# First layer of a two-layer trunk: where the convolution's taps read, who makes the first of them, and which PSUM banks the gate projection uses

## The chip, the cores and the metric

One core of a Trainium2 chip runs the whole program in one launch. Its engines work side by side, each through its own list of instructions in order: TensorE (PE, matmuls), VectorE (DVE), ScalarE (ACT), GpSimd (POOL), and SyncE (SP), whose queue issues the DMAs. SBUF is the on-chip memory, and matmul results land in PSUM, which has eight banks of 128 x 512 float32. GpSimd's operations of this kernel work in SBUF alone. The metric is the device time of one execution in microseconds (us); the figure that counts is the median of the runs.

## The reference

The input is 2048 frames of 1024 channels. The first layer is a gated linear recurrence, the second a gated delta rule; each has a norm scaled by a conditioning vector before it and a gated residual behind it. The change touches the first layer only, but for where one constant is made:

```python
def rglru_block(h, in_w, conv_w, conv_b, gate_w, gate_b, lam, out_w):
    proj = h @ in_w                                   # 1024 -> 2 x 1024
    xb, zg = proj[..., :D_RNN], proj[..., D_RNN:]
    xb = causal_dwconv(xb, conv_w) + conv_b           # 4 taps along the frames, each channel by itself
    ...
    pre = jnp.einsum('bsni,knij->kbsnj', xg, gate_w)  # 8 blocks of 128 x 128, two gates
    ...
    y = hseq.astype(h.dtype) * jax.nn.silu(zg)
    return y @ out_w
```

`causal_dwconv` pads three zero frames on the left, so that frame t takes channels of frames t-3 to t.

## The kernel before

**Tiling.** Everything is float32. Channels lie on the 128 partitions, frames along the free dimension. The frames go in two halves `u` of 1024, each in two pieces `i` of 512. A projection weight panel is 1024 x 128 (eight tiles `k`). Weights and activations are split into two parts (`whi`, `wlo`; `hh`, `hl`), and a product takes three passes, so a job (one panel, one piece) is 24 matmuls of 128 x 512 into one PSUM bank (`products`, L667). The first layer has 16 panels: for each block `n` of 128 channels an `x` panel (goes through the convolution) and a `z` panel (the gate projection of the change: SiLU of it multiplies the branch). For a block the jobs run x i=0, x i=1, z i=0, z i=1.

**The convolution** (`conv1_thread`, with `extend` and `taps`): ACT copies the bank into an SBUF tile `xe` of 4 + 512 columns (L727); POOL fills the first four from the piece before (`carry`, L725, or zeros, L721) and saves the last four (L730); POOL makes the first tap with the bias (L741); DVE adds the other three taps (L715). Then `gates_thread`: ACT rounds `xf` to `xh` (L765), DVE makes the rest `xl` (L768), PE multiplies both with the gate weights (`pg`, L774, six matmuls for a piece), ACT and DVE make the gates (L824, L784 to L801), DVE scans along the frames (L805), POOL multiplies by `tz` (L812), which `z1_thread` made (ACT L750, DVE L752).

**PSUM.** Eight banks, two to a tag: `mm` (all projections), `tp` (transposes), `c` (gates), `d` (transposes of the first two pieces, then idle until the second layer's recurrence).

**What sets the order.** A planner (`Weave`) runs threads written as generators. A thread yields what it needs: an event, a buffer slot (`slots[...]`), or an engine for an estimated time (`STT` 0.665 us for a tap, `EV` 0.605, `CP` 0.48). The planner always lets the thread go on that can start earliest by these estimates, and the instructions are issued in that order on each engine. Estimates decide only the order; on the chip each engine follows its list and waits on semaphores. Between the first layer's work lie other threads: norms of the second half (L452 to L459, POOL L245, L246), its transposes by DVE (L506), conditioning rows (DVE L412, `acc`), the split of weights on POOL (L649, `wlo`). At about 505 us the output projection (`mmo`) begins, at 696 us the second layer's projections.

**The second layer's** convolution uses the same `extend` and `taps` and isn't changed. `middle` is a 128 x 128 constant for its decay sums.

## Time and profile before

| | |
|---|---|
| three runs | 1982.22, 1986.4, 1989.81 us; median 1986.4 |
| profiled execution | 1980.38 us, span of its instructions 1978.6 us |
| PE busy | 1846.2 us (93%), 10286 matmuls |
| DVE busy | 1475.7 us (75%) |
| ACT busy | 1046.7 us (53%) |
| POOL busy | 724.1 us (37%) |
| first layer's projections | about 50 to 516 us |
| output projection of the first layer | to 696 us |
| second layer | to the end |

Busy is the time in which an engine has an instruction in work. A busy PE is not PE at its peak: its matmuls are pipelined, and one at the lower clock counts as longer. "PEclk" is the granted share of PE's full clock. An idle gap before an instruction is put down to the engine whose semaphore came last. `xt_d`, `araw`, `raw` and the like are DMA targets of other threads.

### The profile page before, as it was taken

What the parts mean: (1) busy time and instruction counts of PE and PEld (TensorE: products, weight loads), DVE (VectorE), ACT (ScalarE), POOL (GpSimd) and SP (SyncE); (2) the same over time, 40 slices, a digit from 0 to 9 for tenths busy, and PEclk for the clock granted to TensorE, in tenths of its full rate; (3) what the DMA queues carried; (4) which work ended last, traced back from release to release, by engine and by line L of the source; (5) the groups of instructions that cost most, each with busy time, mean ns of one, the idle gap of its engine ahead of it and who ended that gap; (6) DMA issues with size and microseconds to landing.
All of it is one profiled execution on the core that took longest, in us unless ns stands there. A gap on an engine that the chain in (4) does not pass through costs nothing.

```text
span 1978.6 us, 31398 instructions
## 1 busy us (share of the span) xinstructions
PE 1846.2 (93%) x10286; PEld 1500.3 (76%) x10286; DVE 1475.7 (75%) x3171; ACT 1046.7 (53%) x2555; POOL 724.1 (37%) x1215
## 2 busy tenths in 40 slices
PE   6998889999998998898989999999999999999998
PEld 3776667787787777777777778777888888878887
DVE  6788798887644567778977898567778778877654
ACT  3655567666411236465555555555656566654321
POOL 4555664444200135345344544333333334311101
PEclk9999999999999999999999999999999999999999
DMA  8355655654578724547764457455465555577751
GB/s 334 103 157 158 223 168 169 200 178 153 175 198 210 225 74 140 145 114 176 189 161 130 119 125 191 128 147 147 119 152 147 131 133 140 149 219 221 225 186 64
DMA packets 511724, 322.77 MB, mean 163 GB/s; under 512 B 371268, under 2 KB 439236, under 8 KB 511560
## 3 DMA queue, kind: packets, MB, share of 16 engines
q1 hardware_dynamic: 511560, 320.77, 57.4%
q8 instruction: 81, 1.33, 0.3%
q14 instruction: 83, 0.68, 0.1%
HBM read 219.93 MB, written 100.73 MB: 162 GB/s over the span
## 4 chain that ended last, share of the span: by engine, by line
PE 46%; DVE 21%; DMA 10%; issue 6%; ACT 6%; POOL 5%; SPq 5%; DVEq 0%; POOLq 0%; ACTq 0%
PE mm L667 21%; PE mmo L667 12%; DVE xf L715 6%; DMA raw<-in_w 2%; DVE ttmp L1249 2%; DVE tblk L1252 2%; PE pg L774 1%; DMA xt<-x_d 1%; SPq L1187 1%; SPq L512 1%; DVE acc L412 1%; PE pp L1369 1%; PE pS L1398 1%; PE pkk L1129 1%; PE pS L1399 1%
## 5 line engine op out<-in xcount | busy, mean ns | idle before, releaser
L715 DVE SCALAR_TENSOR_TENSOR xf<-xe,cw_s,xf 128x512 f32<-128x512 f32 x384 | 331.4, 866 | 46.7 <-POOL xf L958 24.1
L649 POOL TENSOR_TENSOR wlo<-raw,whi 128x1024 fp32r<-128x1024 f32 x48 | 120.6, 2512 | 99.7 <-ACT whi L643 81.2
L1249 DVE TENSOR_TENSOR ttmp<-blk,tblk 128x60 f32<-128x60 f32 (+24 forms) x496 | 118.3, 238 | 24.9 <-DMA blk<-blk_d 11.5
L643 ACT CAST whi<-raw 128x1024 fp32r<-128x1024 f32 x96 | 100.4, 1045 | 64.5 <-DMA raw<-in_w 54.7
L1252 DVE TENSOR_TENSOR tblk<-tblk,ttmp 128x60 f32<-128x60 f32 (+24 forms) x496 | 122.3, 247 | 10.0 <-POOL tblk L1243 0.2
L730 POOL COPY carry<-xe 128x4 f32<-128x4 f32 x128 | 40.3, 315 | 239.2 <-ACT xe L727 237.1
L727 ACT COPY xe<-mm 128x512 f32<-128x512 f32 x128 | 73.9, 578 | 74.0 <-PE mm L667 73.0
L667 PE MATMUL mm<-hh_('in2', 0)_5201,whi 128*128 128x512 f32 x256 | 105.0, 410 | 4.1 <-ACT xe L727 4.1
L667 PE MATMUL mmo<-oh,yh 128*128 128x512 f32 x256 | 101.1, 395 | 7.8 <-DVE xr L922 7.2
L667 PE MATMUL mm<-hh_('in2', 1)_12203,whi 128*128 128x512 f32 x256 | 105.2, 411 | 2.8 <-ACT xe L727 2.8
L667 PE MATMUL mm<-hh_('in2', 0)_5424,whi 128*128 128x512 f32 x256 | 103.7, 405 | 2.1 <-ACT xe L727 1.5
L667 PE MATMUL mm<-hh_('in2', 0)_5201,wlo 128*128 128x512 f32 x256 | 105.3, 411 | 0.0
L667 PE MATMUL mm<-hl_('in2', 0)_5425,whi 128*128 128x512 f32 x256 | 104.9, 410 | 0.0
L667 PE MATMUL mm<-hl_('in2', 0)_5202,whi 128*128 128x512 f32 x256 | 104.6, 409 | 0.0
L667 PE MATMUL mm<-hh_('in2', 1)_12379,wlo 128*128 128x512 f32 x256 | 104.4, 408 | 0.0
L667 PE MATMUL mm<-hh_('in2', 1)_12203,wlo 128*128 128x512 f32 x256 | 104.4, 408 | 0.0
L667 PE MATMUL mm<-hh_('in2', 0)_5424,wlo 128*128 128x512 f32 x256 | 104.0, 406 | 0.0
L667 PE MATMUL mm<-hl_('in2', 1)_12204,whi 128*128 128x512 f32 x256 | 103.8, 405 | 0.0
L667 PE MATMUL mm<-hl_('in2', 1)_12380,whi 128*128 128x512 f32 x256 | 103.2, 403 | 0.0
L667 PE MATMUL mm<-hh_('in2', 1)_12379,whi 128*128 128x512 f32 x256 | 103.1, 403 | 0.0
L667 PE MATMUL mmo<-oh,oh 128*128 128x512 f32 (+1 forms) x264 | 102.0, 386 | 0.2 <-DVE tz L986 0.2
L667 PE MATMUL mmo<-ol,oh 128*128 128x512 f32 (+1 forms) x264 | 102.1, 387 | 0.0
(324 smaller groups left out, 5698.7 us busy)
## 6 DMA issues: line engine op xcount, KB each, us to landing
raw<-in_w SPq DMA_DIRECT2D x96, 512.0 KB, 4.2
araw<-in_ada_w SPq DMA_DIRECT2D x32, 512.0 KB, 4.4
xt<-x_d SPq DMA_DIRECT2D x32, 512.0 KB, 4.5
xt_d<-xb SPq DMA_DIRECT2D x192, 64.0 KB, 2.6
xk<-xt_d SPq DMA_DIRECT2D x24, 512.0 KB, 5.5
xt<-in_x SPq DMA_DIRECT2D x16, 512.0 KB, 4.9
ada<-in_ada_w SPq DMA_DIRECT2D x16, 512.0 KB, 9.1
y_d<-tz SPq DMA_DIRECT2D x32, 256.0 KB, 3.1
```

What stands on the lines that cost most here:

```text
L412: dve.scalar_tensor_tensor(acc, raw[:, k, :], ck, acc, ALU.mult, ALU.add)
L512: sp.dma_start(out=dst[c_], in_=tb[32 * c_:32 * c_ + 32])
L643: act.copy(hi, raw)
L649: pool.tensor_tensor(lo, raw, f(hi), ALU.subtract)
L667: pe.matmul(pt, lhsT=lhs[a][:, k, :], rhs=rhs[b][:, k, :], start=(k == 0 and n == 0), stop=(k == KT - 1 and n == 2))
L715: dve.scalar_tensor_tensor(xf, xe[:, 1 + j:1 + j + TC], wc[:, j:j + 1], xf, ALU.mult, ALU.add)
L727: act.copy(xe[:, 4:4 + TC], pt)
L730: pool.tensor_copy(out=carry, in_=xe[:, TC:TC + 4])
L774: pe.matmul(pg, lhsT=a[:, g, :], rhs=b, start=(q == 0), stop=(q == 2))
L1129: pe.matmul(pkk[:, b, :], lhsT=kc, rhs=kc, start=True, stop=True)
L1249: dve.tensor_tensor(tmp, blk[:, j, j + 1:32].unsqueeze(2).to_broadcast([P, r, c_]), t[:, j, 0:c_].unsqueeze(1).to_broadcast([P, r, c_]), A ...
L1252: dve.tensor_tensor(t[:, j + 1:32, 0:c_], t[:, j + 1:32, 0:c_], tmp, ALU.subtract)
```

## The change

A new function `convolve` takes the place of `extend`, POOL's first tap and `taps` in the first layer. ACT makes the tap that needs no earlier frame (the last weight, with the bias) straight from PSUM into `xf`, for the columns 3 to 511. It then copies the first three and the last three columns of the bank into a small buffer `edge1`, six columns for each piece and channel block. DVE adds the other three taps from PSUM into columns 3 to 511; the bank is free after the third. The first three columns of the piece come apart, from the six edge columns that lie side by side in `edge1`: one product of 3 x 4, one sum over 4, one addition of the bias. `xe1` and `carry1` go; the rounding `xh`, which shared `xe1`'s buffers, gets its own tag `xh`. The `z` jobs of the first layer take the tag `d` in place of `mm`. `middle` is made when the second layer's buffers are opened, no longer at the start.

```diff
-    middle = cp.tile([P, P], F32, name="middle")
-    pool.tensor_copy(out=middle, in_=upper)
-    pool.tensor_scalar(middle[0:64, :], middle[0:64, :], -1.0, 0.0, ALU.add, ALU.add)
...
-        mtok = yield slots["mm"]
-        pt = ps.tile([P, TC], F32, tag="mm", name="mm")
+
+        bank = "d" if layer == 1 and kind == "z" else "mm"
+        mtok = yield slots[bank]
+        pt = ps.tile([P, TC], F32, tag=bank, name="mm")
...
-    def conv1_thread(u, n, i, pt, mtok):
-        etok = yield slots["xe1"]
-        xe = tile_([P, TC + 4], "xe1", "xe1")
+    def window(ap, *steps):
+        return bass.AP(ap.tensor, ap.offset, [ap.ap[0], *steps])
+
+    def convolve(xf, pt, mtok, wc, bias, edge, key, g, bank):
+
+
+        yield "act", 0.66 if bias is not None else 0.57, 0.0
+        if bias is None:
+            act.activation(xf[:, 3:TC], pt[:, 3:TC], AF.Copy, scale=wc[:, 3:4])
+        else:
+            act.activation(xf[:, 3:TC], pt[:, 3:TC], AF.Identity, bias=bias, scale=wc[:, 3:4])
+        yield "act", 0.18, 0.1
+
+        if g < S // TC - 1:
+            act.copy(edge[:, 6 * g + 3:6 * g + 9].rearrange("p (a b) -> p a b", b=3), window(pt[:, 0:3], (TC - 3, 2), (1, 3)))
+        else:
+            act.copy(edge[:, 6 * g + 3:6 * g + 6], pt[:, 0:3])
+        w.set(ev("edge", key, g))
+        for j in range(3):
+            yield "dve", STT, 0.13 if j < 2 else 0.05
+            dve.scalar_tensor_tensor(xf[:, 3:TC], pt[:, j:j + TC - 3], wc[:, j:j + 1], xf[:, 3:TC], ALU.mult, ALU.add)
+        put(bank, mtok)
+        if g > 0:
+            yield ev("edge", key, g - 1)
+        etok = yield slots["ed"]
+        yield "dve", 0.09, 0.1
+        pr = tile_([P, 3, 4], "ed", "ed")
+        dve.tensor_tensor(pr, window(edge[:, 6 * g:6 * g + 3], (1, 3), (1, 4)), wc.unsqueeze(1).to_broadcast([P, 3, 4]),
+                          ALU.mult)
+        yield "dve", 0.09, 0.1
+        dve.tensor_reduce(out=xf[:, 0:3], in_=pr, axis=mybir.AxisListType.X, op=ALU.add)
+        if bias is not None:
+            yield "dve", 0.14, 0.1
+            dve.tensor_scalar(xf[:, 0:3], xf[:, 0:3], bias, None, ALU.add)
+        put("ed", etok)
+
+    def conv1_thread(u, n, i, pt, mtok, bank):
         yield ev("columns")
-        yield from extend(xe, pt, mtok, carry1[:, n, :], ("x", n), u * NTC + i)
         ftok = yield slots["xf1"]
-        yield "pool", 0.76
         xf = tile_([P, TC], "xf1", "xf1")
-        pool.tensor_scalar(xf, xe[:, 1:1 + TC], cw1_s[:, n, 0:1], cb1_s[:, n:n + 1], ALU.mult, ALU.add)
-        yield from taps(xe, xf, cw1_s[:, n, :])
-        put("xe1", etok)
+        yield from convolve(xf, pt, mtok, cw1_s[:, n, :], cb1_s[:, n:n + 1], edge1[:, n, :], ("x", n), u * NTC + i, bank)
...
+        middle = tile_([P, P], "middle", "middle")
+        pool.tensor_copy(out=middle, in_=upper)
+        pool.tensor_scalar(middle[0:64, :], middle[0:64, :], -1.0, 0.0, ALU.add, ALU.add)
+        w.set(ev("middle"), middle)
         w.set(ev("l2"))
...
+        edge1 = tile_([P, KT, 6 * (S // TC)], "edge1", "edge1")
+        pool.memset(edge1, 0.0)
```

The new estimates make the planner order the whole first layer anew. Three places follow. Lines of the changed kernel differ from those of before (L663 for L667, L751 for the taps L715, L796 for `xl` L768, L802 for L774, L820 for L792, L840 for L812, L489 for L493).

On DVE, the two pieces of block 2 of the first half; of before, `xf_1041` and `xf_1077` are the pieces i=0 and i=1, `xb` is a transpose of the second half's frames:

```order
L715 SCALAR_TENSOR_TENSOR xf_1041<-xe_992,cw_s,xf_1041 128x512
L801 TENSOR_TENSOR tg<-tg 128x512
L715 SCALAR_TENSOR_TENSOR xf_1041<-xe_992,cw_s,xf_1041 128x512
L805 SCALAR_TENSOR_TENSOR tg<-th,hcar,tg 128x512
L715 SCALAR_TENSOR_TENSOR xf_1041<-xe_992,cw_s,xf_1041 128x512
L715 SCALAR_TENSOR_TENSOR xf_1077<-xe_1048,cw_s,xf_1077 128x512
L506 STREAM_TRANSPOSE xb<-xt 128x512
L715 SCALAR_TENSOR_TENSOR xf_1077<-xe_1048,cw_s,xf_1077 128x512
L768 TENSOR_TENSOR xl<-xf_1041,xh 128x512
L715 SCALAR_TENSOR_TENSOR xf_1077<-xe_1048,cw_s,xf_1077 128x512
```

Of the changed kernel, the same pieces are `xf_1009` and `xf_1064`; `ed` is the product of the edge columns:

```order
L751 SCALAR_TENSOR_TENSOR xf_1009<-mm,cw_s,xf_1009 128x509 x3
L758 TENSOR_TENSOR ed<-edge_123,cw_s 128x12
L761 TENSOR_REDUCE xf_1009<-ed 128x3
L764 TENSOR_SCALAR xf_1009<-xf_1009,cb_s 128x3
L829 TENSOR_TENSOR tg<-tg 128x512
L833 SCALAR_TENSOR_TENSOR tg<-th,hcar,tg 128x512
L751 SCALAR_TENSOR_TENSOR xf_1064<-mm,cw_s,xf_1064 128x509
L796 TENSOR_TENSOR xl<-xf_1009,xh 128x512
L751 SCALAR_TENSOR_TENSOR xf_1064<-mm,cw_s,xf_1064 128x509 x2
L758 TENSOR_TENSOR ed<-edge_123,cw_s 128x12
L761 TENSOR_REDUCE xf_1064<-ed 128x3
```

The three taps of i=0 stand together, the edge operations follow them, and `xl` of i=0 stands behind one tap of i=1 in place of two taps and a transpose.

On POOL at the same two pieces, before (`tz` is the last product of an earlier piece, `wlo` the split of a panel):

```order
L649 TENSOR_TENSOR wlo<-raw_938,whi 128x1024
L730 COPY carry_103<-xe_992 128x4
L741 TENSOR_SCALAR xf_1041<-xe_992,cw_s,cb_s 128x512
L725 COPY xe_1048<-carry_103 128x4
L808 COPY hcar<-tg 128x1
L842 TENSOR_TENSOR gl<-gw,gh 128x256
L812 TENSOR_TENSOR tz<-tz,tg 128x512
L730 COPY carry_103<-xe_1048 128x4
L741 TENSOR_SCALAR xf_1077<-xe_1048,cw_s,cb_s 128x512
L808 COPY hcar<-tg 128x1
L812 TENSOR_TENSOR tz<-tz,tg 128x512
```

And of the changed kernel, the same stretch:

```order
L645 TENSOR_TENSOR wlo<-raw_953,whi 128x1024
L836 COPY hcar<-tg 128x1
L840 TENSOR_TENSOR tz<-tz,tg 128x512
L870 TENSOR_TENSOR gl<-gw,gh 128x256
L836 COPY hcar<-tg 128x1
L840 TENSOR_TENSOR tz<-tz,tg 128x512
L645 TENSOR_TENSOR wlo<-raw_1068,whi 128x1024
L241 TENSOR_SCALAR ss<-ss 128x1
```

No operation of the convolution is left on POOL between the `wlo` of two panels; the others stay.

On PE at the layer's start, where the second piece's frames are transposed (`tph`) between the first products; before, the places around the first gate products (`pg`):

```order
L493 MATMUL tph<-ident,xt 128x128 x4
L667 MATMUL mm<-hl_('in1', 0)_481,whi 128x512
L667 MATMUL mm<-hh_('in1', 0)_480,wlo 128x512
L667 MATMUL mm<-hh_('in1', 0)_480,whi 128x512
L667 MATMUL mm<-hl_('in1', 0)_481,whi 128x512
L667 MATMUL mm<-hh_('in1', 0)_480,wlo 128x512
L667 MATMUL mm<-hh_('in1', 0)_480,whi 128x512
L667 MATMUL mm<-hl_('in1', 0)_481,whi 128x512
L667 MATMUL mm<-hh_('in1', 0)_480,wlo 128x512
L774 MATMUL pg<-xh,gh 128x512
L774 MATMUL pg<-xl,gh 128x512
L774 MATMUL pg<-xh,gl 128x512
```

And of the changed kernel:

```order
L663 MATMUL mm<-hh_('in1', 0)_471,whi 128x512
L663 MATMUL mm<-hl_('in1', 0)_472,whi 128x512
L663 MATMUL mm<-hh_('in1', 0)_471,wlo 128x512
L489 MATMUL tph<-ident,xt 128x128 x12
L802 MATMUL pg<-xh,gh 128x512
L802 MATMUL pg<-xl,gh 128x512
L802 MATMUL pg<-xh,gl 128x512
L489 MATMUL tph<-ident,xt 128x128 x4
L802 MATMUL pg<-xh,gh 128x512
L802 MATMUL pg<-xl,gh 128x512
L802 MATMUL pg<-xh,gl 128x512
L489 MATMUL tph<-ident,xt 128x128 x4
```

Before, the last group of four transposes stood behind the 55th product of the layer. Now 20 transposes stand behind the 57th, with the first gate products between them, because these transposes take turns on the banks `tp` and `d`, and the first `z` job holds one of `d`.

From the first jobs of the output projection on, the rows of all engines stand as before but for a few: the two operations for `middle` on POOL, and a single product or pair of products on PE that changes places with a neighbour.

## Rows read from the trace of the kernel before

**Rows 1.** Stretches of the span: busy us (instructions) of each engine, PEclk, DMA share, GB/s.
```profile
50.00:100.00 50.00, 46.26 (x212) 36.55 (x212) 39.91 (x53) 32.02 (x47) 26.47 (x31) 0.99 0.38 103
100.00:350.00 250.00, 219.65 (x894) 172.86 (x893) 211.54 (x245) 157.82 (x217) 143.00 (x138) 0.95 0.57 176
350.00:450.00 100.00, 98.04 (x440) 80.06 (x439) 87.53 (x112) 65.58 (x87) 45.17 (x52) 1.00 0.56 179
450.00:516.00 66.00, 64.01 (x274) 50.71 (x272) 51.05 (x60) 42.05 (x53) 29.53 (x31) 1.00 0.48 158
516.00:696.00 180.00, 170.66 (x734) 137.78 (x733) 93.04 (x128) 42.34 (x53) 18.91 (x26) 0.99 0.72 207
696.00:1979.00 1283.00, 1217.02 (x7639) 1004.32 (x7637) 959.85 (x2502) 688.06 (x2070) 439.61 (x904) 0.99 0.56 149
```

**Rows 2.** What PE waited for, 100 to 350 us: us in total, times, longest.
```profile
PE pg L774 <- DVE xl L768: 20.0, 8, 5.2
...
PE mm L667 <- DVE tz L752: 0.4, 1, 0.4
```

**Rows 3.** Chain of waits, 119 to 137 us: start us, us, what.
```profile
117.70 1.70 POOL tz L812
...
120.00 2.28 POOL xf L741
...
126.93 0.61 DVE xl L768
...
129.24 1.28 PE pg L774 x3
...
133.55 0.70 PE pg L774 x3
```

**Rows 4.** Instructions in order of time, DVE and then POOL: start us, us, operation.
```profile
122.30 1.87 DVE L715 SCALAR_TENSOR_TENSOR xf<-xe,cw_s,xf 128x512 f32<-128x512 f32 x1 [0.51 <-POOL xf L741]
...
124.73 2.21 DVE L715 SCALAR_TENSOR_TENSOR xf<-xe,cw_s,xf 128x512 f32<-128x512 f32 x1
...
127.46 0.74 DVE L715 SCALAR_TENSOR_TENSOR xf<-xe,cw_s,xf 128x512 f32<-128x512 f32 x1
...
123.59 2.79 POOL L649 TENSOR_TENSOR wlo<-raw,whi 128x1024 fp32r<-128x1024 f32 x1
```

**Rows 5.** Taps and `tz`, 50 to 516 us: ns min/median/max, first and last start.
```profile
L715 DVE SCALAR_TENSOR_TENSOR xf<-xe,cw_s,xf x96: 705/752/2896, 58.4 to 507.7; 128x512 f32<-128x512 f32 x96
...
L752 DVE SCALAR_TENSOR_TENSOR tz<-tz,mm x32: 655/680/690, 61.4 to 507.1; 128x512 f32<-128x512 f32 x32
```

**Rows 6.** DVE's groups, 100 to 350 us: busy us, mean ns, idle before and releaser.
```profile
L715 DVE SCALAR_TENSOR_TENSOR xf<-xe,cw_s,xf 128x512 f32<-128x512 f32 x48 | 53.0, 1105 | 8.0 <-POOL xf L741 7.7
L412 DVE SCALAR_TENSOR_TENSOR acc<-araw,c_col,acc 128x512 f32<-128x512 f32 x24 | 23.3, 973 | 1.4 <-DMA araw<-in_ada_w 1.2
L794 DVE SCALAR_TENSOR_TENSOR tg<-tg,xf 128x512 f32<-128x512 f32 x17 | 18.6, 1094 | 0.0
...
L752 DVE SCALAR_TENSOR_TENSOR tz<-tz,mm 128x512 f32<-128x512 f32 x17 | 11.6, 681 | 8.4 <-ACT tz L750 5.6 <-issue 2.8
```

**Rows 7.** POOL's groups, 50 to 516 us, columns as in rows 6.
```profile
L741 POOL TENSOR_SCALAR xf<-xe,cw_s,cb_s 128x512 f32<-128x512 f32 x32 | 40.1, 1254 | 0.8 <-DVE tg L794 0.6
...
L730 POOL COPY carry<-xe 128x4 f32<-128x4 f32 x32 | 15.7, 492 | 16.9 <-ACT xe L727 16.7
...
L725 POOL COPY xe<-carry 128x4 f32<-128x4 f32 x24 | 13.0, 542 | 2.2 <-DVE xf L715 2.2
```

**Rows 8.** ACT's groups: 40 to 520 us, and the last row the whole span.
```profile
L727 ACT COPY xe<-mm 128x512 f32<-128x512 f32 x32 | 18.7, 583 | 44.8 <-PE mm L667 44.6
...
L562 ACT ACTIVATE h<-tph,cond 128x512 f32<-128x512 f32 x12 | 8.7, 776 | 10.8 <-DVE cond L271 6.7 <-PE tph L493 3.0 <-POOL hl_('in1', 0)_481 L573 1.1
...
L1030 ACT COPY ab<-pb 128x64 f32<-128x64 f32 x4 | 0.8, 204 | 2.2 <-PE pb L1027 2.2
```

**Rows 9.** A small DVE operation, 50 to 516 us, columns as in rows 6.
```profile
L274 DVE SCALAR_TENSOR_TENSOR cond<-cond,norm_s 128x4 f32<-128x4 f32 x2 | 0.3, 160 | 0.0
```

More of the change, by code (lines that the diff above doesn't have):

```diff
@@ L193, in trunk_kernel @@
     dtb_s = cp.tile([P, NH], F32, name="dtb_s")
-    carry1 = cp.tile([P, KT, 4], F32, name="carry1")
     hcar = cp.tile([P, KT], F32, name="hcar")
@@ L210, in trunk_kernel @@
         "gs": 2, "eg": 2}.items()}
-    for t in ("xe", "xf", "vt", "ec", "gr", "ab", "gin", "gg", "spe", "spd"):
+    for t in ("xe", "xf", "vt", "ec", "gr", "middle", "ab", "gin", "gg", "spe", "spd"):
         tags[t] = ("l2a", tags[t][1])
@@ L685, in job @@
         if layer == 1:
-            w.spawn((conv1_thread if kind == "x" else z1_thread)(u, m, i, pt, mtok), 2, 0.2)
+            w.spawn((conv1_thread if kind == "x" else z1_thread)(u, m, i, pt, mtok, bank), 2, 0.2)
         elif kind == "z":
@@ L744, in conv1_thread, with z1_thread @@
         w.set(ev("xf", u, n, i), (xf, ftok))
-    def z1_thread(u, n, i, pt, mtok):
+    def z1_thread(u, n, i, pt, mtok, bank):
         ztok = yield slots["tz"]
@@ L752, in z1_thread @@
         dve.scalar_tensor_tensor(tz, tz, 1.0, pt, ALU.add, ALU.mult)
-        put("mm", mtok)
+        put(bank, mtok)
         w.set(ev("tz", u, n, i), (tz, ztok))
@@ L758, in gates_thread @@
         gh, gl = yield ev("gw", u, n)
-        etok = yield slots["xe1"]
+        etok = yield slots["xh"]
         ltok = yield slots["xr"]
@@ L763, in gates_thread @@
         yield "act", CP
-        xh = tile_([P, TC], "xe1", "xh", F32R)
+        xh = tile_([P, TC], "xh", "xh", F32R)
         act.copy(xh, xf)
@@ L775, in gates_thread @@
             w.spawn(gate_thread(u, n, i, g, pg, ctok), 3)
-        put("xe1", etok)
+        put("xh", etok)
         put("xr", ltok)
@@ L1045, in decay_thread @@
         yield "pe", 1.1
+        middle = yield ev("middle")
         pgc = ps.tile([P, 3, NB * NH], F32, tag="tp", name="pgc")
```

7 lines of the change are left out of this document (4 added, 3 removed).

## Prediction

> **What bounds the kernel now.** I read the busy times in stretches first [rows 1]. The change touches only the first layer's projections, 50 to 516 us; the question there is how fast TensorE (PE) issues. From 350 to 450 us it issues 440 matmuls in 100 us, 4.40 per us, at full granted clock. At that rate the 894 matmuls of 100 to 350 us need 203.2 us, so that stretch loses 46.8 of its 250 us; the 212 of 50 to 100 need 48.2 (1.8 lost), the 274 of 450 to 516 need 62.3 (3.7 lost). All the change can win here is about 52 us. Behind 516 us the instructions stand as before on every engine (but for a few rows), so those 1460 us are taken as unchanged.
>
> What costs the 46.8 us? In PE's waits [rows 2], gate products waiting for `xl` on VectorE (DVE) are the one large entry, 20.0 us in 8 waits, 2.5 us each. The rest is mostly what follows them: in the chain of waits [rows 3] the gate products after such a wait take 0.43 us each (1.28 for three), and 4 us later 0.23 (0.70 for three), which are TensorE's two clock levels, 1.2 and 2.4 GHz; the stretch's mean granted clock is 0.95 [rows 1]. So DVE sets PE's pace from 100 to 350 us, where it is busy 211.5 of 250 us.
>
> The same piece of chain shows why `xl` is late. GpSimd (POOL) does `tz` of an earlier piece and then the first tap `xf` (L741, 2.28 us) of piece i=1; only then DVE's taps of that piece may run, and `xl` of the finished piece i=0 stands behind two of them in DVE's order. The time order of both engines [rows 4] adds a second cause: a tap that starts with POOL idle takes 0.74 us; one that meets a POOL operation takes 1.87 us, and the one at 124.73 ends at 126.94, after `wlo` on POOL ended at 126.38. Over the layer a tap takes 705 ns at least, 752 in the median and 2896 at most [rows 5]: the excess is waiting for POOL. The `tz` operation (L752) has the same form with one input in PSUM, and takes 655 to 690 ns, never more.
>
> **The change, part by part**, for the 16 convolutions (48 taps) of 100 to 350 us.
>
> (a) The taps read PSUM in place of `xe`. Today 53.0 us, 1105 ns each [rows 6]. The new operation isn't in the trace. Its nearest rows are L752 with its PSUM input (680) and the undisturbed tap with its column scalar (752, [rows 5]); I take 740, near the second since the scalar stays a column. 48 x (1105 - 740) = 17.5 us less. Bounds: 48 x (1105 - 680) = 20.4 us, and nothing if they are still held.
>
> Here a rule speaks against the change. The Trainium skill, "VectorE: DVE Perf Modes", section "Rules for kernel authors", advises for work on a matmul's output to copy it to SBUF first if many operations follow, and its cycle table gives a VectorE operation from PSUM 62 cycles more than one from SBUF, 65 ns at the 0.96 GHz it states. By that, as an estimate, a tap costs some 65 ns more, 3.1 us for 48, and the sum would be 17 instead of 20 us. The trace disagrees: 680 ns with a PSUM input, against 752 for the SBUF tap [rows 5].
>
> (b) DVE's wait for POOL's first tap, 8.0 us [rows 6], goes; the first tap now waits for the scalar engine (ACT). The `tz` row shows what that can be: 5.6 us put down to ACT for 17. I take half of the 8.0 back: 4 us less, bounds 8 and 0.
>
> (c) Three small DVE operations per convolution make the first three columns. The nearest row is a 128x4 operation, 160 ns [rows 9]: 16 x 3 x 0.16 = 7.7 us. The product has two SBUF inputs, as a tap has, so it can still be held: a tap's mean hold is 1105 - 752 = 0.35 us. POOL loses L741, L730 and L725, 68.8 us [rows 7] of its 244.2 us in 50 to 516 us [rows 1], 28%; 16 x 0.35 x 0.72 = 4.0. Together 12 us more. Bounds: 7.7 (no holds) and 20 (all three held).
>
> (d) The other DVE operations meet that much less POOL work. The rows of `acc` and `tg` L794 [rows 6] stand at 973 and 1094 ns against 752 and 680 undisturbed: 24 x 0.22 + 17 x 0.41 = 12 us of holds; 28% of it is 3.5 us less. Bounds 0 and, with the groups not shown, 8.
>
> (e) DVE so gets back 17.5 + 4 + 3.5 - 12 = 13 us. The chain also gets shorter outside DVE: before a first tap stood an ACT copy (583), the `carry` copy (492) and L741 (1254), now one ACT pass. Its nearest row, the same activation with column scale and bias out of PSUM, takes 776 ns [rows 8]. That is 1.5 us sooner for each convolution. PE waits for `xl` 8 times, so up to 12 us; DVE is busy most of that time, and I take 5. Bounds 0 and 12.
>
> (f) Outside this stretch at most 5.5 us are lost; I take 3 us less. At the start the gate projection holds a `d` bank that transposes of the second half took: five groups of four now stand behind the 57th product of the layer (the last one stood behind the 55th before), with the first gate products among them. Half of the first stretch's loss again, 1 us more; bounds 0 and 4.
>
> (g) Costed at nothing: ACT's longer pass and its edge copy (nearest row 204 ns), 16 x (0.776 - 0.583 + 0.204) = 6.4 us, hidden by ACT's 92 idle us of the 250; uncovered they are 6 us. The `mm` bank, now held through three taps: with `z` on `d` it is wanted again three jobs later, 72 products or 16.4 us, against about 3 us of ACT and taps; without that room the excess would be PE's wait. The bank that `z` leaves alone: PE waits for it once, 0.4 us [rows 2], so the two extra banks win nothing by themselves. The two POOL operations for `middle`, moved to the second layer's start, are covered by POOL's idle time (439.6 of 1283 us busy); POOL's larger L741 takes 1254 ns [rows 7], so uncovered they are 2.5 us at most.
>
> **Sum.** 13 + 5 + 3 - 1 = 20 us less. The profiled execution took 1980.4 us (span 1978.6), which makes 1960; the runs' median of 1986.4 lies 6 us above it, so the median should be **1966 us**.
>
> **Rivals.**
> 1. *PE gets its full pace.* With POOL out of the chain no `xl` is late, and the clock stays up. For it: in 350 to 450 us PE keeps 4.40 per us with DVE at 88% [rows 1]. Against it: that stretch has neither norms nor transposes for DVE; at full pace 100 to 350 us would ask nearly 200 us of DVE in 203. Gain 32 to 52 us, about 40: 1946 us. Chance 0.20.
> 2. *The small operations eat the gain.* Bounds of (c) at 20 and (b) and (e) at nothing: 17.5 + 3.5 - 20 = 1 us, plus 2 outside: 1983 us, no change. For it: the product keeps two SBUF inputs, and each of the three waits for the one before. Against it: POOL has 28% less to do. Chance 0.14.
> 3. *Taps from PSUM are dear*, so that copying first was right. It cancels the gain on DVE when a tap takes 740 + 13000/48 = 1010 ns. Then only (e) and (f) are left, 7 us: 1979 us. Against it: L752's 690 ns at most. Chance 0.04. The skill's rule quoted under (a) is this case; its own figure, an estimate of 805 ns a tap, would leave 1969 us.
> 4. *Slower: ACT waits for a free `xf`.* `xf` has two buffers, let go by `tg` L794 late in the gates. POOL waited for them (0.6 us in all, [rows 7]); now ACT does, and behind it on ACT stand `xh`, the tanh and exp of gates, `whi`, for which DVE and PE wait. If each of the 16 waits as long as PE's gate products do now, 2.5 us, that is 40 us: 1986 - 20 + 40 = 2006 us. It decides from 1.9 us a convolution on. Against it: POOL's 0.6 us, with L741 reaching that point no earlier than ACT will now by 1.5 us. Chance 0.10.
>
> **How the numbers follow.** My forecast's own chance is 0.52 (gain 10 to 32 us). No change means within 0.5%, 10 us, about what a measurement of this kernel can tell. Faster: the forecast and rival 1, and part of 3, 0.75. Same: rival 2 and part of 3, 0.15. Slower: rival 4, 0.10. The range goes to 1944 (rival 1's middle) and up to 1984, where rival 2 ends; beyond lie rival 4 and the far part of rival 1, about 0.2.
>
> **What would show it.** (a) Taps at 720 to 770 ns, at most near 800; (b) no DVE wait for POOL in taps; (c) three rows of 32 with 0.15 to 0.5 us each; (d) `acc` and L794's means nearer 750 and 690; (e) PE's waits for `xl` halved, the projections ending 18 to 25 us sooner than 516, the clock of 100 to 350 us nearer 1. A wait of ACT's `xf` for DVE `tg`, or small operations over 0.5 us, would make the prediction wrong; so would a later stretch that gives the gain back, above all the output projection from 516 to 696 us, where PE and the DMAs are both near their limits (171 of 180 us, 0.72).

## The result and the profile after

The changed kernel takes 1976.1 us (median of 11 runs, 1969.6 to 1981.7) against 1984.9 us (11 runs, 1978.8 to 1990.8) for the kernel before on the same chip: ratio 0.995, interval 0.9934 to 0.9966, or 9 us less. The forecast was 20 us less (1966 us). The direction is right and the size about half. The profiled execution took 1977.2 us with a span of 1975.5 us; that of before took 1980.4.

Stretches of the span after, columns as in [rows 1]; the third is the first layer from 50 us to its last gate product, the fourth the second layer from its first product to the end, the fifth a piece of the final projection:

```profile
100.00:350.00 250.00, 228.86 (x962) 181.70 (x961) 219.72 (x310) 167.25 (x242) 102.83 (x91) 0.97 0.62 193
350.00:450.00 100.00, 99.02 (x434) 79.76 (x433) 84.11 (x132) 70.21 (x98) 30.73 (x29) 1.00 0.54 174
50.00:498.50 448.50, 423.42 (x1807) 338.01 (x1807) 378.90 (x559) 301.56 (x433) 169.13 (x153) 0.98 0.55 171
679.60:1975.50 1295.90, 1225.02 (x7639) 1006.29 (x7637) 959.88 (x2502) 687.97 (x2070) 438.60 (x906) 0.99 0.56 148
1890.00:1960.00 70.00, 70.00 (x303) 56.76 (x302) 34.83 (x40) 14.66 (x31) 6.76 (x20) 1.00 0.34 106
```

The last three of them in the kernel before:

```profile
50.00:516.20 466.20, 428.17 (x1815) 340.36 (x1815) 390.03 (x467) 297.47 (x403) 244.16 (x251) 0.97 0.54 167
695.90:1978.60 1282.70, 1217.12 (x7639) 1004.42 (x7637) 959.85 (x2502) 688.06 (x2070) 439.61 (x904) 0.99 0.56 149
1890.00:1960.00 70.00, 70.00 (x310) 57.98 (x310) 34.65 (x40) 14.68 (x31) 6.38 (x18) 1.00 0.39 120
```

The first thing to see: the last gate product ends at 498.5 in place of 516.2 us, 17.7 us sooner, and the second layer's first product starts at 679.6 in place of 695.9 us, 16.3 us sooner. That is nearly the whole forecast. (In a second pair of profiles, below, that product came 12.5 us sooner.) The second: from there to the end the kernel takes 1295.9 in place of 1282.7 us, 13.2 us longer, with the same 7639 matmuls and a granted clock that reads 0.99 in both. PE is busy 7.9 us longer and idle 5.3 us longer. The gain was made where it was foretold, and most of it was given back in a part that the prediction took as unchanged.

The third is how that part can get slower. In the final projection PE is busy all the time at full granted clock in both kernels, and does 310 matmuls in 70 us before, 303 after: 226 and 231 ns each. The stretch from 350 to 450 us has it too: 434 matmuls in 99.02 busy us, where 440 took 98.04 [rows 1]. The matmuls of one pair of tiles in the final projection, ns min/median/max, before and then after:

```profile
L667 PE MATMUL mmo<-ol,oh x104: 389/389/389, 1889.8 to 1959.9; 128*128 128x512 f32 x104
```
```profile
L663 PE MATMUL mmo<-ol,oh x101: 390/393/404, 1889.7 to 1959.4; 128*128 128x512 f32 x101
```

Not every product of the changed kernel is slower. The first line below is the same projection earlier, 1830 to 1865 us, when its `oh` and `ol` panels still lie in the tiles of the weight panels. The other two are products of the first layer's second half with the same weight panels `whi`, piece 0 and then piece 1, 285 to 479 us:

```profile
L663 PE MATMUL mmo<-oh,oh x52: 389/389/389, 1830.0 to 1864.7; 128*128 128x512 f32 x52
```
```profile
L663 PE MATMUL mm<-hh_('in1', 1)_1785,whi x124: 389/393/477, 285.0 to 479.0; 128*128 128x512 f32 x124
...
L663 PE MATMUL mm<-hh_('in1', 1)_2280,whi x112: 387/389/405, 296.4 to 467.7; 128*128 128x512 f32 x112
```

VectorE after, 50 to 516 us: the taps' durations in ns (min/median/max) as in [rows 5], and then groups with the columns of [rows 6]:

```profile
L751 DVE SCALAR_TENSOR_TENSOR xf<-mm,cw_s,xf x96: 700/742/752, 59.0 to 490.7; 128x509 f32<-128x509 f32 x96
```
```profile
L751 DVE SCALAR_TENSOR_TENSOR xf<-mm,cw_s,xf 128x509 f32<-128x509 f32 x96 | 70.7, 739 | 14.4 <-ACT edge L747 7.6 <-ACT edge L745 5.7
...
L796 DVE TENSOR_TENSOR xl<-xf,xh 128x512 fp32r<-128x512 f32 x32 | 34.9, 1092 | 7.2 <-ACT xh L793 6.8
...
L764 DVE TENSOR_SCALAR xf<-xf,cb_s 128x3 f32<-128x3 f32 x32 | 7.6, 236 | 0.4
...
L758 DVE TENSOR_TENSOR ed<-edge,cw_s 128x12 f32<-128x12 f32 x32 | 5.5, 171 | 0.0
L761 DVE TENSOR_REDUCE xf<-ed 128x3 f32<-128x12 f32 x32 | 5.0, 157 | 0.3
```

None of the 96 taps that read PSUM is held: 752 ns at most, where the SBUF tap went up to 2896. But `xl`, which has two SBUF inputs, now takes 1092 ns in the mean. In the kernel before it was:

```profile
L768 DVE TENSOR_TENSOR xl<-xf,xh 128x512 fp32r<-128x512 f32 x32 | 24.3, 763 | 7.7 <-ACT xh L765 7.4
```

PE's waits, 100 to 350 us, answer to [rows 2]:

```profile
PE pg L802 <- DVE xl L796: 17.8, 10, 5.5
```

The longest of them in order of time:

```profile
245.62 2.34 POOL L645 TENSOR_TENSOR wlo<-raw,whi 128x1024 fp32r<-128x1024 f32 x1
...
245.98 2.53 DVE L796 TENSOR_TENSOR xl<-xf,xh 128x512 fp32r<-128x512 f32 x1
...
248.57 0.80 PE L802 MATMUL pg<-xl,gh 128*128 128x512 f32 x1 [5.53 <-DVE xl L796]
```

`xl` starts beside `wlo` on POOL, 0.36 us behind it, and ends only at 248.51, after `wlo` (247.96). The hold that fell on a tap before falls on `xl` now, and on `xl` PE waits directly. The Trainium skill, "SBUF — State Buffer", section "SBUF: two separate sides", tells of an exclusive lock on a port pair that VectorE and GpSimd share: a VectorE operation with two SBUF inputs contends there with a GpSimd operation that reads SBUF, and whichever starts second waits for the whole of the first. Taps with one SBUF input at 700 to 752 ns and the 2.53 us of `xl` agree.

Last, the scalar engine (ACT). Its groups, 50 to 516 us:

```profile
L741 ACT ACTIVATE xf<-mm,cb_s,cw_s 128x509 f32<-128x509 f32 x32 | 24.8, 774 | 35.0 <-PE mm L663 26.2 <-DVE tg L822 8.6
L745 ACT COPY edge<-mm 128x6 f32<-128x6 f32 x24 | 3.8, 156 | 0.0
```

It waited 8.6 us for a free `xf` (rival 4's wait), in 4 places.

### The profile page after: what moved, and what is told of

Its sections match the earlier page's. It is cut to its first block, busy times and chain, and to the rows that moved or that the text cites. A ratio compares the mean times of both kernels' runs of the same rounds, so it can differ in the third digit from the quotient of the medians.

```text
span 1975.5 us, 31410 instructions
## 1 busy us (share of the span) xinstructions
PE 1851.2 (94%) x10286; PEld 1501.2 (76%) x10286; DVE 1468.9 (74%) x3267; ACT 1052.4 (53%) x2587; POOL 649.4 (33%) x1120
## 4 chain that ended last, share of the span: by engine, by line
PE 45%; DVE 19%; DMA 13%; ACT 8%; issue 7%; SPq 5%; POOL 3%; DVEq 0%; POOLq 0%; ACTq 0%
PE mm L663 23%; PE mmo L663 12%; DVE xf L713 3%; DMA pq<-q_d 2%; DMA raw<-in_w 2%; DVE tblk L1286 2%; SPq L1221 2%; PE pg L802 2%; DVE ttmp L1283 1%; ACT junkq L1201 1%; DMA vn<-v_d 1%; DVE xf L751 1%; DMA q_d<-tb 1%; DMA ada<-in_ada_w 1%; DMA oraw<-in_ow 1%
## 5 line engine op out<-in xcount | busy, mean ns | idle before, releaser
L663 PE MATMUL mm<-hh_('in2', 0)_5231,whi 128*128 128x512 f32 x256 | 105.4, 412 | 4.3 <-ACT xe L725 4.3
L663 PE MATMUL mm<-hh_('in2', 1)_12236,whi 128*128 128x512 f32 x256 | 105.1, 411 | 2.6 <-ACT xe L725 2.6
L663 PE MATMUL mm<-hh_('in2', 0)_5454,whi 128*128 128x512 f32 x256 | 104.0, 406 | 2.2 <-ACT xe L725 1.9
L663 PE MATMUL mmo<-oh,yh 128*128 128x512 f32 x256 | 101.5, 397 | 4.4 <-DVE xr L950 4.4
L663 PE MATMUL mm<-hl_('in2', 0)_5455,whi 128*128 128x512 f32 x256 | 105.3, 411 | 0.0
L663 PE MATMUL mm<-hh_('in2', 0)_5231,wlo 128*128 128x512 f32 x256 | 104.9, 410 | 0.0
L663 PE MATMUL mm<-hl_('in2', 0)_5232,whi 128*128 128x512 f32 x256 | 104.7, 409 | 0.0
L663 PE MATMUL mm<-hh_('in2', 1)_12236,wlo 128*128 128x512 f32 x256 | 104.5, 408 | 0.0
L663 PE MATMUL mm<-hh_('in2', 0)_5454,wlo 128*128 128x512 f32 x256 | 104.5, 408 | 0.0
L663 PE MATMUL mm<-hh_('in2', 1)_12412,wlo 128*128 128x512 f32 x256 | 104.4, 408 | 0.0
L663 PE MATMUL mm<-hl_('in2', 1)_12237,whi 128*128 128x512 f32 x256 | 103.9, 406 | 0.0
L663 PE MATMUL mm<-hl_('in2', 1)_12413,whi 128*128 128x512 f32 x256 | 103.3, 403 | 0.0
L663 PE MATMUL mm<-hh_('in2', 1)_12412,whi 128*128 128x512 f32 x256 | 103.2, 403 | 0.0
L663 PE MATMUL mmo<-oh,oh 128*128 128x512 f32 (+1 forms) x264 | 102.7, 389 | 0.2 <-DVE tz L1019 0.2
L663 PE MATMUL mmo<-ol,oh 128*128 128x512 f32 (+1 forms) x264 | 102.9, 390 | 0.0
L663 PE MATMUL mmo<-oh,ol 128*128 128x512 f32 (+1 forms) x264 | 102.5, 388 | 0.0
L663 PE MATMUL mmo<-oh,yl 128*128 128x512 f32 x256 | 101.2, 395 | 1.2 <-DVE yl L924 1.2
```

Source lines behind the costliest of these rows:

```text
L663: pe.matmul(pt, lhsT=lhs[a][:, k, :], rhs=rhs[b][:, k, :], start=(k == 0 and n == 0), stop=(k == KT - 1 and n == 2))
```

## The experiments

Theory at the start: the first layer won what was foretold; the loss behind 680 us comes from the program, where the new tiles moved other tiles in SBUF. Rivals: it is the scatter of executions, or it comes from the two extra banks. A product reads a 128 x 128 piece of a panel and a 128 x 512 piece of a larger tile; the larger tiles lie in three places of SBUF, slots A, B and C. The panels lie in the weight panels' tiles (`whi`, `wlo`) or, in the output projections, in tiles of their own, here called output panels (`yh`, `yl` and later `oh`, `ol`). The compiled programs show the move: in the changed kernel the weight panels and slots A and B lie 640 bytes lower than before, and slot C, the output panels and the second layer's tiles 512 bytes lower. So the distance from the weight panels to slot C is 12416 bytes where it was 12288, and that from slot A to the nearest output panel of the final projection 82304 where it was 82176: 128 bytes more in both. In the table "first product" is the second layer's and "rest" is from it to the end, both of the profiled execution; the ratio is to the kernel before on the same chip.

| run | median us | ratio (interval) | first product | rest |
|---|---|---|---|---|
| before, profile of step one | | | 695.9 | 1282.7 |
| the change | 1976.1 | 0.995 (0.9934 to 0.9966) | 679.6 | 1295.9 |
| before, again | 1983.0 (one run) | | 695.2 | 1286.0 |
| the change, again | 1977.6 | 0.9971 (0.9953 to 0.9989) | 682.7 | 1302.1 |
| z on mm | 1980.7 | 0.9975 (0.9960 to 0.9991) | 686.0 | 1293.1 |
| banks alone | 2000.8 | 1.0078 (1.0047 to 1.0109) | 713.0 | 1286.8 |
| old places | 1977.0 | 0.9932 (0.9913 to 0.9951) | 684.3 | 1290.3 |
| new places | 1997.2 | 1.0031 (1.0017 to 1.0045) | 699.1 | 1291.5 |
| split low half | 1981.1 | 0.995 (0.993 to 0.997) | 696.4 | 1287.2 |
| no edges | 1970.7 | 0.9894 (0.9875 to 0.9914) | 676.9 | 1288.0 |
| gap of 128 | 1992.0 | 1.0035 (1.0022 to 1.0049) | 698.4 | 1295.3 |
| even shift | 1974.4 | 0.9949 (0.9931 to 0.9967) | 678.2 | 1294.7 |
| bias column | 1981.3 | 0.9978 (0.9962 to 0.9993) | 687.8 | 1286.6 |
| ACT first tap | 1975.9 | 0.9959 (0.9944 to 0.9974) | 685.3 | 1287.9 |

**Both kernels again**, unchanged.

> The kernel before once more, for a second profile. In the profiles so far the change brings the second layer's first product 16.3 us forward (695.9 to 679.6 us), but the last instruction only 3.1 us: 13 us are given back behind 696 us, where the order of instructions is the same. Theory A, the loss is of the execution, not of the program: this profile's second layer (first product to end of span, 1282.7 us in the first profile of before, 1295.9 in that of the changed kernel) takes anything between these, and the median step between matmuls from 1900 to 1965 us (227 ns before, 232 changed) varies as well. Theory B, the program is the cause (other addresses, other moments of the DMAs): 1283 us again, within 2 us, and 227 ns.

> The changed kernel once more. Time: 0.995 of before, as it was. Theory A (execution): its second layer takes another time than 1295.9 us, as near to 1283 as to 1296. Theory B (program): 1296 us again, within 2 us. Either way the second layer's first product comes at 680 us, within 2 us.

The kernel before repeats its second layer within 4 us and its final pace of 227 ns; the changed kernel repeats 231 to 232 ns. So the slower matmuls belong to the program. Executions of the changed kernel do scatter: 6 us in this stretch between its two profiles, and its second profile missed both ranges given for it (682.7 and 1302.1 us).

**The banks apart from the convolution.** With the new convolution, `z` back on `mm`:

```
-        bank = "d" if layer == 1 and kind == "z" else "mm"
+        bank = "mm"
```

> The changed kernel with the gate projection back on the mm banks; the convolution stays new. My prediction has it that the two more banks win nothing while the bank is let go soon, and that they give room to a bank that is now held through three taps. Theory 1: without them TensorE waits for the bank (mm for a tap or for tz), the projections end 5 to 15 us later than 498.5 us, and the time is 0.997 to 1.003 of before. Rival: the three taps end early enough in any case; then the projections end within 3 us of 498.5, and the time is 0.995 of before.

And the old convolution with that line the other way:

> The kernel before with the gate projection on the d banks alone; the convolution stays old. Theory 1 (as predicted): nothing to win, since TensorE waited 0.4 us in all for a bank: projections end at 514 to 518 us, time 0.998 to 1.002 of before, with some 1 us lost at the start to the transposes that share d. Rival: the planner uses the room to place the gate products later and fewer waits for xl are left: projections end 5 us or more before 516, time under 0.998.

What PE waits for, 50 to 715 us, first with the new convolution and `z` on `mm`, then with the banks alone:

```profile
PE mm L663 <- DVE xf L751: 16.9, 6, 4.8
PE pg L802 <- DVE xl L796: 6.2, 8, 1.6
```

```profile
PE pg L775 <- DVE xl L769: 29.4, 13, 5.3
...
PE mmo L667 <- ACT oh L875: 3.7, 1, 3.7
```

The banks alone make the kernel 15 us slower: the waits for `xl` grow (23.1 us before in the same stretch), the output projection meets a new one of 3.7 us, and the granted clock from 516 to 700 us is 0.95 (0.99 before). With the new convolution they are worth 3 to 6 us of the first layer by the profiles (first product 686.0 against 679.6 and 682.7), which the timed runs can't tell from nothing. So theory 1 of the first run was met at the near end of its ranges (its gate products end at 504.1 us), and its mechanism is there: without the two banks PE waits 16.9 us for a bank that a tap still reads, while its waits for `xl` are 6.2 us (18.4 in the changed kernel). Of the second run neither theory had such a loss. The rest of the second layer stays at 1293 us without them, so they are not the cause of the loss behind.

**Addresses, both ways.** The change with everything outside the first layer's pool where it was (`middle` back among the constants, 128 bytes left empty, the edge columns in two state tiles that the first layer doesn't use, `ed` in the first layer's pool):

```
+    middle = cp.tile([P, P], F32, name="middle")
...
+    room = cp.tile([P, KT, 4], F32, name="room")
...
-        edge1 = tile_([P, KT, 6 * (S // TC)], "edge1", "edge1")
+        edge1 = [states[n // 5][:, 24 * (n % 5):24 * (n % 5) + 24] for n in range(KT)]
```

> The changed kernel with every SBUF tile outside the first layer's pool at the address that it has in the kernel before: the 512 bytes of middle go back to the constants, 128 bytes are left empty where carry1 was, the edge columns lie in two of the state tiles (which the first layer does not use) and the products tile of the edges moves into the first layer's pool. The instructions and their order on the engines are the changed kernel's. Theory A, the addresses set the pace of TensorE's operand reads: matmuls of the first layer's projections between 350 and 490 us and of the last 80 us step by 227 ns as before instead of 231 to 232, from the second layer's first product to the end 1283 to 1287 us instead of 1293 to 1302, second layer's first product at 679 or earlier, in all 0.988 to 0.992 of the kernel before (about 1965 us). Rival B, the pace comes from the order or from which banks are written and not from addresses: steps of 231 to 232 ns, 1293 to 1302 us, 0.994 to 0.998.

The kernel before with the changed kernel's addresses:

```
-    middle = cp.tile([P, P], F32, name="middle")
...
-    carry1 = cp.tile([P, KT, 4], F32, name="carry1")
...
-            "ss": ("xp", 4), "rs": ("xp", 4)}
+            "ss": ("xp", 4), "rs": ("xp", 4), "ed": ("xp", 2)}
...
+    tags |= {"carry1": ("l1", 1)}
...
+        if (u, n) == (0, 0):
+            pool.memset(tile_([P, 3, 4], "ed", "ed"), 0.0)
...
+        middle = tile_([P, P], "middle", "middle")
```

> The kernel before with the changed kernel's SBUF addresses: middle is made at the second layer's start in its pool, carry1 moves into the first layer's pool, and two tiles of 64 bytes stand where the changed kernel has its edge products; nothing else changes, the banks and the convolution are those of before. Theory A (addresses): steps of 231 to 232 ns in place of 227, from the second layer's first product to the end 1293 to 1302 us in place of 1283 to 1287, first layer some 3 to 5 us longer (962 products between 100 and 350 us and 434 up to 450 us at 4 ns more), in all 1.006 to 1.010. Rival B (order or banks): 227 ns, 1283 to 1287 us, 0.999 to 1.001.

Their final stretches, first the change at the old addresses, then the kernel before at the new:

```profile
1890.00:1960.00 70.00, 70.00 (x311) 57.96 (x310) 34.92 (x41) 14.69 (x31) 7.33 (x21) 1.00 0.35 106
```
```profile
1890.00:1960.00 70.00, 70.00 (x303) 56.81 (x303) 37.20 (x42) 14.66 (x31) 6.40 (x18) 1.00 0.48 152
```

The pace goes with the addresses: 311 matmuls in 70 us at the old ones, 303 at the new, whichever convolution and banks. In the untouched kernel the new addresses cost 6 us timed (0.31%), half of what theory A gave; in the profiles 3.2 us up to the second layer's first product and 8.8 behind it (3.9 and 5.5 against the second profile of before). In the changed kernel the return is less than theory A gave: 0.9932 where it expected 0.988 to 0.992, 1290.3 us behind the first product where it expected 1283 to 1287, and the first layer came no sooner.

**Which property of the addresses.** The kernel before with only the weight panels and slots A and B 128 bytes lower:

```
-    carry1 = cp.tile([P, KT, 4], F32, name="carry1")
...
-            "ss": ("xp", 4), "rs": ("xp", 4)}
+            "ss": ("xp", 4), "rs": ("xp", 4), "ed": ("xp", 2)}
...
+    tags |= {"carry1": ("l1", 1)}
...
+        if (u, n) == (0, 0):
+            pool.memset(tile_([P, 3, 4], "ed", "ed"), 0.0)
```

> The kernel before with one thing moved: the pools that hold the weight panels and slots A and B lie 128 bytes lower (carry1 moved into the first layer's pool), and two unused tiles of 64 bytes fill the gap, so that slot C, the output stages' panels and the second layer's tiles keep their addresses. The distance from the weight panels to slot C becomes 12416 bytes, as in the changed kernel, where it was 12288. Theory R, the distance between the tiles that a matmul reads sets its pace: the last 80 us step by about 232 ns as in the changed kernel, 350 to 490 us by about 230, and the total is 1.001 to 1.005 of the kernel before. Rival S, the address of the tile itself does (slot C on a multiple of 512 bytes): 227 ns everywhere as before, ratio 0.999 to 1.001.

And the change with every pool 640 bytes lower:

```
-            "ss": ("xp", 4), "rs": ("xp", 4), "ed": ("xp", 2)}
+            "ss": ("xp", 4), "rs": ("xp", 4), "ed": ("l1", 2)}
```

> The changed kernel with only the edge products' tile moved into the first layer's pool, so that every pool behind the constants lies 640 bytes lower than before and all distances between them are those of before. Theory R (distance between the tiles): steps of 227 ns at the end and about 228 from 350 to 490 us, 1284 to 1291 us from the second layer's first product to the end, 0.990 to 0.995 of the kernel before. Rival S (own address): 230 to 232 ns, 1292 us or more, 0.995 to 0.998.

The final stretch of the first, and then of the second:

```profile
1890.00:1960.00 70.00, 70.00 (x304) 56.87 (x303) 38.05 (x43) 13.93 (x29) 7.12 (x20) 1.00 0.53 166
```
```profile
1890.00:1960.00 70.00, 70.00 (x311) 57.97 (x310) 35.55 (x41) 13.87 (x31) 7.30 (x21) 1.00 0.34 106
```

Theory R holds for the pace: 128 bytes more between the tiles slow matmuls though slot C and the output panels lie where they did, and a shift of all by 640 leaves them fast. The traces show it stage by stage. This is the mean step in ns between successive products of a stage (steps of 200 to 260 ns alone, so without waits and without the lower clock):

| stage: panel, larger tile | before | new places | gap of 128 | the change | even shift |
|---|---|---|---|---|---|
| *distance 128 bytes larger in the columns new places, gap of 128 and the change* | | | | | |
| first layer, second half, piece 0: weight panels, slot C | 227.6 | 232.9 | 232.9 | 232.6 | 227.9 |
| its output, first 512 columns: output panels, slot B | 227.4 | 233.1 | 232.8 | 232.9 | 227.4 |
| final projection, panels 8 to 15: output panels, slots A, B | 226.7 | 232.4 | 232.4 | 232.4 | 226.7 |
| *distance as before in all* | | | | | |
| first layer, second half, piece 1: weight panels, slot A | 227.2 | 228.4 | 228.4 | 228.4 | 227.8 |
| its output, other columns: output panels, slot C | 227.0 | 227.4 | 227.7 | 227.3 | 226.9 |
| second layer: weight panels, slots A, B | 229.3 | 229.6 | 229.6 | 229.5 | 229.3 |
| final projection, panels 0 to 7: weight panels' tiles, slots A, B | 227.8 | 228.2 | 228.1 | 228.3 | 228.0 |

The three stages whose distance grew are 5 to 6 ns a product slower; the others, with the same slots and panels in other pairs, are not, or by about 1 ns at most. Each of the three has some 384 products, so at 5.5 ns they cost some 6 us together, an estimate that agrees with the 6 and 7 us timed. Only a third of it lies behind the second layer's first product; with 0.2 to 0.3 ns for each of that layer's 3072 products some 3 us.

The 128 bytes alone cost 0.35%, as much as the whole set of new addresses. The total of the even shift is at the far end of what was expected, and its second layer takes 1294.7 us with fast matmuls, where 1284 to 1291 were expected. Its clock was lower: 30.7 us behind the first product are at the lower granted clock, against 20.5 in the profile of before and 27.3 in that of the change. That alone doesn't set the time: the split low half has 41.0 us of it and takes 1287.2.

**The holds.** At the old addresses, each `wlo` operation cut in four:

```
-                    yield "pool", 2.3
-                    pool.tensor_tensor(lo, raw, f(hi), ALU.subtract)
+                    for k in range(0, KT, 2):
+                        yield "pool", 0.58
+                        pool.tensor_tensor(lo[:, k:k + 2, :], raw[:, k:k + 2, :], f(hi)[:, k:k + 2, :], ALU.subtract)
```

> As the kernel with the old addresses, and each of GpSimd's subtractions that make the low half of a weight panel (128 x 1024, 2.3 us and more) is cut into four of 128 x 256. Theory of the holds: a VectorE operation with two SBUF inputs that starts beside the long subtraction waits until it ends (the operation that makes xl took 1.09 us in the mean, 2.53 us once, while undisturbed ones take about 0.7), so cutting lowers that mean to 0.9 us or less and takes 5 to 10 us of TensorE's 17.8 us of waits for xl: second layer's first product 3 to 8 us earlier than in the kernel with old addresses. Rival: the held time only moves to other operations, or GpSimd's four starts cost it as much as is won: first product within 2 us.

PE's waits there, 50 to 500 us:

```profile
PE pg L804 <- DVE xl L798: 8.4, 6, 2.8
PE pg L804 <- ACT tg L854: 8.3, 4, 3.5
PE pg L804 <- ACT xh L795: 5.9, 3, 3.2
```

`xl` falls from 1039 ns at the old addresses to 771 ns (50 to 516 us), PE's waits for it from 17.6 to 8.4 us (50 to 500 us). So it was `wlo` that held `xl`. But nothing is won: the quarters take 898 ns each, 49.2 us for 14 panels where the whole operation took 40.3 for 16, and PE now waits 5.9 us for `xh` and 8.3 us where the trace names ACT's `tg`; the first product comes 12 us later. The granted clock was lower too, 0.93 from 100 to 350 us against 0.96 at the old addresses. The theory was right on the hold and wrong on its worth.

**The edge columns.** The change without them, so that the first three columns of each piece lack the taps of the frames before it:

```
-            act.activation(xf[:, 3:TC], pt[:, 3:TC], AF.Identity, bias=bias, scale=wc[:, 3:4])
...
-            act.copy(edge[:, 6 * g + 3:6 * g + 9]..., window(pt[:, 0:3], (TC - 3, 2), (1, 3)))
...
+            act.activation(xf, pt, AF.Identity, bias=bias, scale=wc[:, 3:4])
...
-        dve.tensor_tensor(pr, window(edge[:, 6 * g:6 * g + 3], (1, 3), (1, 4)), ..., ALU.mult)
...
-        dve.tensor_reduce(out=xf[:, 0:3], in_=pr, axis=mybir.AxisListType.X, op=ALU.add)
...
-            dve.tensor_scalar(xf[:, 0:3], xf[:, 0:3], bias, None, ALU.add)
```

> The changed kernel without the edge columns: ACT's copy of the six edge columns and VectorE's three small operations on them are left out and ACT's first tap covers all 512 columns, so the first three columns of each chunk lack the taps from the left neighbour. Theory from the changed kernel's rows: 32 convolutions lose 0.56 us of VectorE work each (171 + 157 + 236 ns, 18.1 us in all) and 0.155 us of ACT work; the part that lies on the path between 50 and 500 us is about half, so the second layer's first product comes 8 to 14 us earlier (666 to 672 us) and the total is 0.988 to 0.992 of the kernel before. Rival: VectorE has room for the small operations beside TensorE, and the waits are set by GpSimd's holds: first product less than 4 us earlier.

The first product comes at 676.9 us, 3 to 7 us sooner than in the profiles of the change (679.6, 682.7) and of the change at the old addresses (684.3), less than the expected 8 to 14. This program also has `ed` out of the way, so its distances are those of before, as in the even shift; against that kernel (678.2) it is 1.3 us sooner, as the rival has it. The total, 0.9894, is the lowest of all; the even shift has 0.9949.

With the bias as a fifth column of the edge's products, so that the 236 ns operation goes (at the old addresses; the column is filled once for each panel):

```
+            dve.tensor_copy(out=sums[q][:, :, 4], in_=cb1_s[:, q:q + 1].to_broadcast([P, 3]))
...
-            dve.tensor_scalar(xf[:, 0:3], xf[:, 0:3], bias, None, ALU.add)
```

> The kernel with the old addresses, and the edge's sum takes the bias with it: its products lie in a tile of five columns for each weight panel, whose fifth column holds the bias, made once at the start; so VectorE's third small operation (236 ns, 32 times, 7.6 us) is gone. Theory, the small operations lie on the path as the run without edge columns has it (18.1 us of them and ACT's copy away: second layer's first product 5 to 7 us earlier): a third to a half of that, first product 2 to 4 us earlier than 684.3, total 0.990 to 0.993 of the kernel before. Rival: the waits behind the holds take the place of the operation, first product within 1 us, total as with the old addresses, 0.993.

Neither, but nearer the rival: 7.6 us of VectorE's work are away, and the first product is 3.5 us later, not sooner; the total, 0.9978, is worse than either gave. VectorE only waits more (20.4 us for ACT's `tg` between 50 and 500 us, 5.6 at the old addresses with the operation).

**Only the first tap moves.** The kernel before with one operation on another engine, reading SBUF as before:

```
-        yield "pool", 0.76
+        yield "act", 0.66
...
-        pool.tensor_scalar(xf, xe[:, 1:1 + TC], cw1_s[:, n, 0:1], cb1_s[:, n:n + 1], ALU.mult, ALU.add)
+        act.activation(xf, xe[:, 1:1 + TC], AF.Identity, bias=cb1_s[:, n:n + 1], scale=cw1_s[:, n, 0:1])
```

> The kernel before, and ACT makes the first tap from the extended chunk in SBUF in place of GpSimd; the other taps read SBUF as before, the banks are those of before. Theory: VectorE's taps there need two SBUF inputs and were held beside GpSimd's 1.25 us first tap; without it the 96 taps fall from 1.037 us in the mean to 0.80 to 0.90 us, but ACT's extra pass of about 0.78 us per chunk (31 of them, 24 us) and the remaining holds take part of it back: projections end 5 to 10 us earlier than 516 to 517 us, total 0.994 to 0.998 of the kernel before. Rival: only reading PSUM frees the taps, the other GpSimd operations hold them as much: projections end within 3 us, ratio 0.998 to 1.003.

Its taps, 50 to 516 us, and its first layer:

```profile
L715 DVE SCALAR_TENSOR_TENSOR xf<-xe,cw_s,xf 128x512 f32<-128x512 f32 x96 | 90.2, 942 | 9.1 <-ACT xf L741 7.9
```
```profile
50.00:504.30 454.30, 426.34 (x1811) 339.65 (x1810) 385.08 (x467) 322.31 (x436) 208.41 (x219) 0.97 0.55 170
```

The taps stay long (942 ns; I expected 800 to 900), and still the first layer ends at 504.3 us, 11.8 of the change's 17.7 us sooner, and the total, 0.9959, can't be told from that of the whole change. This kernel keeps the old addresses; the change with its old distances has 0.9932 and 0.9949, lower with intervals that overlap. So taking the first tap from POOL brings two thirds of the first layer's gain. It shortens the chain and it also lessens the holds (the taps took 99.0 us of VectorE before and take 90.2), and this run doesn't part the two.

## Why the prediction was half right

**What bounds, and (a) and (b).** The reading of the first layer held. Taps take 739 ns (740 foretold) and are not held; from 100 to 350 us VectorE's wait ahead of them is 3.6 us for 17 convolutions where 8.0 stood (4 foretold); over the whole layer it is 14.4 us where 17.8 stood. The advice of the Trainium skill ("VectorE: DVE Perf Modes", "Rules for kernel authors") to copy from PSUM first does not hold here: the PSUM tap takes 739 ns, the undisturbed SBUF tap 752 [rows 5].

**(c)** was mis-sized: 171, 157 and 236 ns, 0.56 us a convolution, against 0.75 foretold. Only the product has two SBUF inputs, and it was hardly held.

**(d)** failed in its reasoning. POOL's work fell by the foretold 28% and more (244 to 169 us), but the holds did not fall with it: `xl` went from 24.3 to 34.9 us. Of the two rows named, `acc` stands at 926 ns and `tg` (now L822) at 817 from 100 to 350 us, where 973 and 1094 stood and 750 and 690 were looked for. A hold needs two operations at the same time, and which pairs meet follows from the new order, not from POOL's total alone. All of VectorE's work but taps and edges took 390.0 - 99.0 = 291.0 us before and 378.9 - 70.7 - 18.1 = 290.1 after: what others lost, `xl` took.

**(e)** has the right sum from other terms, which is luck in part. VectorE got back 390.0 - 378.9 = 11 us of work and 76.2 - 69.6 = 7 us of idle time over the layer. But PE's waits for `xl` were to halve and went from 20.0 to 17.8 us: the last hold on `xl` took the place of the late tap. In the prediction the shorter chain was worth 5 us of 18, with bounds 0 and 12; moving the first tap alone gave 11.8 us with taps still at 942 ns, 7.0 of them idle time of VectorE. That makes the chain the likely larger part; it isn't shown apart from the holds.

**(f), (g).** The start lost about what was foretold: from 50 to 100 us PE does 206 matmuls where it did 212. The banks by themselves were costed at nothing. Alone they lose 15 us; beside the new convolution they win at most a few, since the 16.9 us of waits for a bank that they spare come back in part as waits for `xl`. So "two extra banks win nothing by themselves" was too kind, and the two halves of the change can't be added up from each alone.

**The step that failed** is the sentence that "those 1460 us are taken as unchanged" because the instructions stand as before. They do, in number and order, yet the second layer and the output took 13 us longer in the profile. The prediction itself named a later stretch that gives the gain back as a sign against it; it looked to the first layer's output projection, which kept its time (181.1 us from the last gate product to the second layer's first product, 179.7 before). The runs show one cause: the change's smaller constants and its `ed` tiles moved panels and slots by 128 bytes against each other, and the matmuls on such pairs step by 232 to 233 ns where they did by 227. Put alone into the kernel before, that costs 6 to 7 us timed (1.0031 and 1.0035), more than half of the 11 us that are missing from the 20. But more than half of it falls on the first layer and its output, where the gain came through in spite of it; of the 13 us behind, the slower steps explain some 3. Most of the rest is 5.3 us of PE's idle time and, as an estimate, 3 to 4 us of the lower clock (half of the 27.3 us less half of the 20.5).

**What stays open** is why these two grew. The addresses seem to have a hand in it: the five profiles at the new distances took 1291.5 to 1302.1 us behind the first product, the nine at the old ones 1282.7 to 1294.7. But with the fast matmuls back the complete changed kernels had 0.9932, 0.9949, 0.995 and 0.9978, around those of the change as it is (0.995 and 0.9971), so a return is not shown by the timed runs. And their second layer took 1287 to 1295 us, against 1283 to 1288 in kernels with the taps in SBUF and the old distances.

**Rivals.** Rival 1 (PE at full pace) did not come: 962 matmuls in 250 us, where 4.40 per us would be 1100. Rival 2's total (1983) was not reached. Rival 3 is excluded. Rival 4's wait is there, 8.6 us in 4 waits of 32: the sign that was to make the prediction wrong came, too rarely to decide.

No version beats the change by more than the measurement can tell; the change at the old addresses (0.9932) has the lowest ratio among complete kernels, and the move of the first tap alone gives nearly the same as the whole change.

## What to carry to other kernels

Ask first which engine's step stands in the chain, and move that one alone: here one operation moved from GpSimd to ACT gave two thirds of the first layer's gain and a total that can't be told from that of the rewritten convolution. A hold between VectorE and GpSimd goes to whatever meets the long operation next, so look whom it will hit before counting it as won. And when a change adds or removes tiles, compare the distances between the tiles that matmuls read, far away too; a stage whose instructions are the same can still get slower.

## Not expected of the hardware

The pace of a matmul depends on how far apart the two SBUF tiles lie that it reads. With 12288 bytes between the weight panels and slot C, or 82176 between slot A and the final output panels, 128 x 128 by 128 x 512 products step by 227 ns (389 ns long each, minimum, median and maximum in the final projection); with 128 bytes more by 232 to 233 ns (390, 393 and 404 ns there). It is the distance and not the address: one kernel with the larger distance left slot C in place and was slow, one with all tiles 640 bytes lower was fast, and within one kernel products on the same slots are slow or fast by where the other tile lies. Only the 128 bytes more were tried, so which other distances are slow, and what in the chip it is, stays open.
